# A hybrid decoder layer on one core: the split halves of the output and MLP weights are kept in DRAM from the first token block on

## The chip, the cores and the metric

The kernel runs on one core of a Trainium2 chip. The metric is the device time of one execution in microseconds, the median of several runs; the profile shows one execution of its own. The engines are called PE (TensorE, the matmuls; PEld are its weight loads), DVE (VectorE), ACT (ScalarE), POOL (GpSimd) and SP (SyncE, whose queue issues all of this kernel's DMAs).

## The reference, cut to what matters

One layer of a decoder is computed for a prompt of 2048 tokens and, beside it, for 8 sequences of 8 new tokens (the 64 "sample" tokens). All data is fp32. The width is 1024, the MLP's 2816.

```
h = rmsnorm(x, norm_mix) * (1 + sc_m) + sh_m
rq, rk, rv, rg, sq, sk, sv = split(h @ w_in)          # 3584 columns
mix = concat(retention(rq, rk, rv, rg), sb_attention(sq, sk, sv)) @ w_out
x = x + g_m * mix
h = rmsnorm(x, norm_ffn) * (1 + sc_f) + sh_f
a, bval = h @ w_up_gate, h @ w_up_val                 # 2816 columns each
ff = (silu(conv3(a)) * bval) @ w_down
x = x + g_f * ff;  y = rmsnorm(x, norm_final)
```

The shifts, scales and gates come from a small projection of a condition vector. The sample tokens attend to 2048 cached tokens each.

## The kernel before, in words

**Products in three parts.** Every large product is made with operands split in two fp32r halves: `hi` is the operand rounded to fp32r, `lo` the rest. `split` (L173) makes them with one ACT copy (L174) and one DVE subtraction, which stands in the trace under the helper line L159. `mm3` (L293) then issues hi x hi, hi x lo and lo x hi (L295 to L297). Four products with 512 moving columns share a row of weights in the token-major projections; in the feature-major ones a tile of 8 rows meets all 512 tokens of a block, so that one pair of weight halves feeds 24 matmuls of 512 columns. The last block carries the 64 sample tokens too: its feature-major products take 576 columns as two pieces of 288, and its token-major ones add a short tile (L304, L305).

**Weights.** A weight comes from DRAM as `raw`, 1 MiB (in the down projection also 512 KiB), into one of two buffers of the pool `wraw`. `w_split` (L266) turns each half of it into a pair of halves, 512 KiB each, in two of the six slots of the pool `whl`; so three pairs fit. `w_fm` (L272) yields the pairs of two feature-major tiles, `w_tm` (L288) those of two rows of a token-major projection, as they are asked for. There are 74 pairs a block in the four matrices of the change: 8 in `w_out`, 22 each in `w_up_gate` and `w_up_val`, 22 in `w_down`; `w_in` has 28 and the condition's matrix 48 pairs in all, so that there are 74 x 4 + 28 x 4 + 48 = 456 splits. The raw loads of the four matrices are 4, 11, 11 and 14 in a block.

**Blocks and order.** The prompt is cut in four blocks of 512 tokens. The first part of the kernel makes the input projections of all blocks, beside the sample's attention and the retention. Then `out_block(0)` makes the first output projection, and `ffn_block(0)` to `ffn_block(3)` run the MLP. The output projection of the next block runs between the two halves of the last down projection of the present one; at the end of that, the first two gate pairs of the next block are fetched ahead (`first_gates`). The MLPs of blocks 0 to 2 are traced side by side with the prompt's attention for blocks 1 to 3 (`_weave`), which uses PE, ACT, DVE and POOL, and loads keys and values through SP; block 3 runs alone. Inside a block the columns of the MLP come in four parts (6, 6, 6 and 4 tiles of 128), each with its gate, value and down projection.

The framework orders the instructions of each engine, places every tile in a slot of its pool and adds the semaphore waits. Each engine, and SP for the DMAs, works its instructions in order: one that waits holds all behind it. A slot is written anew only when all that read or wrote the earlier tile have ended.

Of the kernel before, what the change touches and what calls it, by code (L numbers as in the profile page):

```python
# [5 lines left out]
F32 = mybir.dt.float32  # L6
F32R = mybir.dt.float32r
# [112 lines left out]
class _Stream:  # L120
    """Traced work in steps; each step yields its share of the whole, or None while it has to wait."""

# [15 lines left out]
def _weave(streams, until=None):  # L138
    """Traces the streams side by side, each at the rate that lets all of them end together."""
    while any(s.live for s in streams) and (until is None or until.live):  # L140
        for s in sorted((s for s in streams if s.live), key=lambda s: s.got / s.total):
            if s.step():
                break
        else:
            raise RuntimeError("streams wait for each other")


def body(tc, I, O):
# [18 lines left out]
    def ld(o, i):  # L167
        dma(sp, o, i)
# [7 lines left out]

    w_in, w_out = I["w_in"][0], I["w_out"][0]
    w_ug, w_uv, w_dn = I["w_up_gate"][0], I["w_up_val"][0], I["w_down"][0]
    xp = I["x_prompt"][0]
# [84 lines left out]

    # ------------------------------------------------------------ weights
    def w_split(src, a, b, eng=dve):  # L266
# [4 lines left out]

    def w_fm(src, c0):  # L272
        raw = T(wraw, [P, 2048], F32, "raw").rearrange("p (a b) -> p a b", a=8)
        ld(raw, src[:, c0 : c0 + 256].rearrange("(k p) c -> p k c", p=P))
        for m in range(2):
            yield w_split(raw[:, :, m * P : (m + 1) * P], 8, P)

# [9 lines left out]

    def w_tm(src, r0, n, c0):  # L288
        for r, raw in w_rows(src, r0, n, c0):
            for q in range(0, raw.shape[1], 2):  # L290
                yield r + q, w_split(raw[:, q : q + 2], 2, 512)

# [6 lines left out]
    def tok_mm(ps, x, w, start, stop):  # L299
        """Rows of tokens x (hi, lo) times w; a short tile has hi and lo side by side, their rows to be added."""  # L300
        if isinstance(x, tuple):
            mm3(ps, x, w, start, stop)
        else:
            pe.matmul(ps, x, w[0], start=start, stop=False)  # L304
            pe.matmul(ps, x, w[1], start=False, stop=stop)  # L305
# [40 lines left out]
    def by_tile(tiles, k0, n):  # L346
        """The products of two rows of weights with the tiles; those of the last two tile after tile."""
        order = [(k, tile) for k in range(k0, k0 + 2) for tile in tiles]
        return sorted(order, key=lambda kt: kt[1]) if k0 == n - 2 else order

    def dense_pair(wts, acts, t, features=False):
        """Two tiles of outputs, the first half of the tokens (or features) of both before the second."""
        outs = [fm_banks(t) for _ in wts]
        for h in range(2):
            for wt, out in zip(wts, outs):
                if features:
                    for ps, c0, c1 in out:
                        fm_chunk(wt, acts, ps[:, : c1 - c0], c0, c1, range(h * 4, h * 4 + 4))
                elif t == 512:
                    fm_chunk(wt, acts, out[0][0][:, h * 256 : h * 256 + 256], h * 256, h * 256 + 256)  # L360
                else:
                    ps, c0, c1 = out[h]
                    fm_chunk(wt, acts, ps[:, : c1 - c0], c0, c1)
        return outs
# [7 lines left out]

    # ------------------------------------------------------------ norms
    def rstd_of(ss, n, scale, p=P):
# [21 lines left out]
    def half_features(x, o, n, kh, A, B, acts, hpool):  # L396
        """Half kh of the columns of normalised rows, scaled and shifted, into columns o.. as hi and lo."""
        ks = slice(kh * 4, kh * 4 + 4)
# [32 lines left out]
    def sb_norm(o, n, pl, gain, tag):  # L431
        """o: [P, n], two heads of 64 rows; returns o / rms of its head * gain. Yields between its steps."""
        w = min(P, n)
# [29 lines left out]

    # ------------------------------------------------------------ preparation
    def prep(pl, kp):
# [100 lines left out]

    # ------------------------------------------------------------ input projection
    def raw_features(hp, xT):
        """The first block's rows, normalised and transposed before the modulation is known."""
        for i, o, n in TILES + [(NT, TB, NS)]:  # L570
# [179 lines left out]

    # ------------------------------------------------------------ decode attention
    def decode(dp):
# [184 lines left out]

    # ------------------------------------------------------------ retention
    def group_norm(ps, gg, qd, pl, n):
        """ps: [n, 512], four heads, each lacking its rows' decay qd; returns the gated norm of the whole."""  # L940
        mv = T(pl, [P, HR, 2], F32, "mv")
# [155 lines left out]

    # ------------------------------------------------------------ prompt attention
    def attention(blocks, tp):
# [102 lines left out]

    # ------------------------------------------------------------ output projection and MLP
    def out_block(g, xpools, fp, samp):
        """Output projection, residual and the MLP's normalised input; xpools() gives the pool of x2."""
        t = TB + (NS if samp else 0)
# [61 lines left out]
    def ffn_block(g, x2, fp, samp, after=None):  # L1268
        """The MLP and the final norm; `after` runs between the halves of the last down projection."""
        t = TB + (NS if samp else 0)  # L1270
# [123 lines left out]
    def conv_state(fi, fp):  # L1394
        """The last rows of two tiles of gates, as rows."""
        s = T(fp, [P, 512], F32, "hf")
        ps = pz()
        for q in range(2):
            cs = T(fp, [P, 18], F32, "cvc")
            pool.tensor_copy(cs[:, 0:2], carry[:, fi + q, :])  # L1400
            pool.tensor_copy(cs[:, 2:18], scarry[:, fi + q].rearrange("p b j -> p (b j)"))
            pe.transpose(ps[:18, q * P : (q + 1) * P], cs, ident)
        act.copy(s[:18, : 2 * P], ps[:18, : 2 * P])
        cs = slice(fi * P, (fi + 2) * P)
        sv(O["conv_state_prompt"][:, cs], s[0:2, : 2 * P])
        sv(O["conv_state_sample"].rearrange("b j d -> (b j) d")[:, cs], s[2:18, : 2 * P])
# [12 lines left out]

    # ------------------------------------------------------------ the parts in their order  # L1420
    tile_pool = lambda name, bufs=1: tc.tile_pool(name=name, bufs=bufs, reuse_waits="tile")
# [85 lines left out]
class _Bufs:  # L1507
    """A pool whose tags have their own numbers of slots."""

# [9 lines left out]
class _Two:  # L1519
    """Two pools, the first for the tags given."""  # L1520

# [44 lines left out]
```

## Time and profile before

| | |
|---|---|
| runs | 3482.68, 3483.96, 3484.57 us; median 3483.96 |
| profiled execution | 3483.6 us, mean granted clock of PE 0.979 |
| last raw load of `w_out` for block 0 issued | 1233.4 us |
| first gate load of block 0 issued | 1265.1 us |
| DMA | 527.72 MB in all, mean 151 GB/s |

In the rows of groups the columns are the line, the engine, the operation, what it writes and reads, shapes and count, then busy time and the mean of one in ns, then the idle time of the engine in front of them and what ended it. In the rows of stretches they are the stretch and its length, the busy time of each engine with the number of instructions, the granted share of PE's clock, the busy share of the 16 DMA engines and the GB/s moved; where a tile is asked for, only the instructions that read or write it are counted. In the rows of waits a line gives who waited for whom, the time in total, how often, and the longest. In the rows of the timeline and of the chain: start, duration, engine, line and tiles. `whl` are the halves of weights, `raw` a weight as loaded, `act` the halves of a block's activations, `ahl` and `abe` attention's tiles, `hf`, `c`, `a` and `ff` those of the MLP, `gp` a gate of the residual.

### The profile page before, as it was taken

To read this page: it belongs to the slowest core of one execution; us is meant where nothing else is said; L and a number is where in the kernel's file an instruction comes from. 1 tells how busy PE (TensorE), PEld (TensorE's weight loads), DVE (VectorE), ACT (ScalarE), POOL (GpSimd) and SP (SyncE) were. 2 spreads that over 40 slices of the span, in tenths; PEclk is the share of its full clock that TensorE was granted. 3 is DMA by queue.
4 is the path that set the end of the run, shared out by engine and by line. 5 is a ranking of instruction groups with operands and counts; after the bars stand their busy time and mean duration, and the time that the engine had idled before them with its cause. 6 is when DMAs were issued, how large, how long until landed. Compare 5 with 4: busy or idle time off the path is not lost. (4 is left out here: it accounts for less than half of the span.)

```text
span 3483.6 us, 49595 instructions
## 1 busy us (share of the span) xinstructions
PE 3298.8 (95%) x17111; PEld 2693.4 (77%) x17111; DVE 2287.1 (66%) x3258; ACT 1777.9 (51%) x3153; POOL 1021.5 (29%) x1898
## 2 busy tenths in 40 slices
PE   7999999899999989999998999998899999899998
PEld 5887877776777768777877778777677777799997
DVE  5466666665665567777768777776877775545445
ACT  5457666554544456455556555554655553433323
POOL 3012011101433243434344333333433323221113
PEclk8999999999999989999999999999999999999999
DMA  6666776666756763443453333335333334332221
GB/s 226 229 198 193 234 230 218 221 223 211 210 178 194 246 196 103 121 121 112 121 182 118 118 118 112 106 112 181 109 118 106 112 103 136 112 107 88 83 86 65
DMA packets 406233, 527.72 MB, mean 151 GB/s; under 512 B 27830, under 2 KB 244009, under 8 KB 405982
## 3 DMA queue, kind: packets, MB, share of 16 engines
q1 hardware_dynamic: 405982, 524.55, 47.8%
q8 instruction: 136, 2.23, 0.3%
q14 instruction: 115, 0.94, 0.1%
HBM read 442.47 MB, written 81.99 MB: 151 GB/s over the span
## 5 line engine op out<-in xcount | busy, mean ns | idle before, releaser
L159 DVE TENSOR_TENSOR whl<-raw,whl 128x1024 fp32r<-128x1024 f32 x456 | 572.7, 1260 | 566.8 <-ACT whl L174 556.5
L174 ACT CAST whl<-raw 128x1024 fp32r<-128x1024 f32 x456 | 477.3, 1050 | 909.2 <-PE d L296 639.0
L295 PE MATMUL d<-act,whl 128*128 128x512 f32 (+2 forms) x2016 | 741.9, 369 | 5.5 <-ACT act L424 4.7
L297 PE MATMUL d<-act,whl 128*128 128x512 f32 (+2 forms) x2016 | 737.9, 366 | 4.6 <-DVE whl L159 4.6
L296 PE MATMUL d<-act,whl 128*128 128x512 f32 (+2 forms) x2016 | 735.7, 365 | 4.2 <-POOL act L159 2.2
L295 PEld LDWEIGHTS d<-act,whl 128*128 128x128 f32 x2016 | 385.8, 192 | 66.0 <-ACT act L424 6.7
L297 PEld LDWEIGHTS d<-act,whl 128*128 128x128 f32 x2016 | 385.4, 191 | 65.0 <-DVE whl L159 5.9
L296 PEld LDWEIGHTS d<-act,whl 128*128 128x128 f32 x2016 | 387.2, 192 | 60.9 <-POOL act L159 2.6
L295 PE MATMUL d<-whl,ff 128*128 128x512 f32 x704 | 280.9, 399 | 0.0
L296 PE MATMUL d<-whl,ff 128*128 128x512 f32 x704 | 280.0, 398 | 0.0
L297 PE MATMUL d<-whl,ff 128*128 128x512 f32 x704 | 279.9, 398 | 0.0
L295 PE MATMUL d<-whl,act 128*128 128x512 f32 x640 | 258.4, 407 | 14.0 <-DVE hf L159 10.8
L296 PE MATMUL d<-whl,act 128*128 128x512 f32 x640 | 259.0, 405 | 0.1
L297 PE MATMUL d<-whl,act 128*128 128x512 f32 x640 | 257.3, 403 | 0.0
L1138 DVE TENSOR_TENSOR_SCAN aom<-aom,acy 128x512 f32<-128x512 f32 x192 | 250.9, 1307 | 5.1 <-ACT aom L1124 4.6
L159 DVE TENSOR_TENSOR abe<-abe,aom 128x512 f32<-128x512 f32 (+2 forms) x320 | 234.3, 732 | 25.9 <-POOL abe L1128 5.1
L1162 PE MATMUL acc<-ahl,avv 128*128 128x512 f32 (+3 forms) x640 | 226.0, 413 | 17.6 <-ACT ahl L174 11.4
L1124 ACT ACTIVATE aom<-z,nb 128x512 f32<-128x512 f32 (+2 forms) x320 | 201.0, 628 | 73.4 <-PE z L1121 57.2
L1121 PE MATMUL z<-akk,aq 128*128 128x512 f32 (+3 forms) x640 | 193.4, 378 | 12.0 <-DVE scd L159 5.8
L1125 ACT ACTIVATE abe<-z,bb 128x512 f32<-128x512 f32 (+2 forms) x320 | 199.7, 624 | 0.0
L159 DVE TENSOR_TENSOR ahl<-z,ahl 128x512 fp32r<-128x512 f32 (+1 forms) x320 | 191.0, 597 | 11.4 <-ACT ahl L174 11.1
L159 POOL TENSOR_TENSOR ff<-ff,hf 128x512 f32<-128x512 f32 (+1 forms) x101 | 160.5, 1611 | 107.8 <-DVE hf L159 107.7
(289 smaller groups left out, 6219.4 us busy)
## 6 DMA issues: line engine op xcount, KB each, us to landing
raw<-in_w_in SPq DMA_DIRECT2D x56, 1024.0 KB
raw<-in_w_up_gate SPq DMA_DIRECT2D x44, 1024.0 KB
raw<-in_w_up_val SPq DMA_DIRECT2D x44, 1024.0 KB
akk<-k SPq DMA_DIRECT2D x160, 256.0 KB
page<-in_cache_k_pages SPq DMA_DIRECT2D x128, 256.0 KB
page<-in_cache_v_pages SPq DMA_DIRECT2D x128, 256.0 KB
raw<-in_w_down SPq DMA_DIRECT2D x32, 1024.0 KB
raw<-in_w_ada SPq DMA_DIRECT2D x24, 1024.0 KB
```

The costliest lines, as they stand in the source:

```text
L159: eng.tensor_tensor(o, a, b, op)
L174: act.copy(hi, src)
L295: pe.matmul(ps, sh, mh, start=start, stop=False)
L296: pe.matmul(ps, sh, ml, start=False, stop=False)
L297: pe.matmul(ps, sl, mh, start=False, stop=stop)
L1121: pe.matmul(z[:, :n], qs[g, h][:, i * P : (i + 1) * P], kk[:, c, :n], start=c == 0, stop=c == 1)
L1124: act.activation(om[:, :n], z[:, :n], AF.Sigmoid, bias=nb[:, h : h + 1], scale=-SCALE)
L1125: act.activation(be[:, :n], z[:, :n], AF.Sigmoid, bias=bb[:, h : h + 1], scale=SCALE)
L1138: dve.tensor_tensor_scan(rv, rv, rv, init, ALU.mult, ALU.bypass)
L1162: pe.matmul(accs[0][:, cs], kv[u][1][:, kt, :], m[:, cs], start=(s == g and kt == 0 and c == 0), stop=(s == 0 and kt == NT - 1 and c == 1),)
```

## The change

In block 0 each pair of halves of `w_out`, `w_up_gate`, `w_up_val` and `w_down` is written to a DRAM tile of its own (`keep`: two stores of 512 KiB). In blocks 1 to 3, and wherever the pair is asked for again, it is loaded from there into two slots of `whl` (`again`: two loads of 512 KiB); the raw load, the ACT copy and the DVE subtraction are not made. `w_in` and the condition's matrix go on as before. Docstrings and comments were dropped too.

```diff
-    w_in, w_out = I["w_in"][0], I["w_out"][0]
-    w_ug, w_uv, w_dn = I["w_up_gate"][0], I["w_up_val"][0], I["w_down"][0]
+    w_in, w_out, w_ug, w_uv, w_dn = "w_in", "w_out", "w_up_gate", "w_up_val", "w_down"
+    W = {n: I[n][0] for n in (w_in, w_out, w_ug, w_uv, w_dn)}
+    KEPT = (w_out, w_ug, w_uv, w_dn)
+    kept = {}
...
-    def w_fm(src, c0):
+    def keep(key, w):
+
+        if key[0] in KEPT:
+            t = kept[key] = T(dram, [2, P, 1024], F32, "kw")
+            for c in range(2):
+                sv(t[c], w[c].rearrange("p a b -> p (a b)"))
+        return w
+
+    def again(key, a):
+        w = []
+        for c in range(2):
+            t = T(whl, [P, 1024], F32R, "whl")
+            ld(t, kept[key][c])
+            w.append(t.rearrange("p (a b) -> p a b", a=a))
+        return tuple(w)
+
+    def w_fm(name, c0):
+        keys = [(name, c0, m) for m in range(2)]
+        if keys[0] in kept:
+            for key in keys:
+                yield again(key, 8)
+            return
         raw = T(wraw, [P, 2048], F32, "raw").rearrange("p (a b) -> p a b", a=8)
-        ld(raw, src[:, c0 : c0 + 256].rearrange("(k p) c -> p k c", p=P))
-        for m in range(2):
-            yield w_split(raw[:, :, m * P : (m + 1) * P], 8, P)
+        ld(raw, W[name][:, c0 : c0 + 256].rearrange("(k p) c -> p k c", p=P))
+        for m, key in enumerate(keys):
+            yield keep(key, w_split(raw[:, :, m * P : (m + 1) * P], 8, P))
...
-    def w_tm(src, r0, n, c0):
-        for r, raw in w_rows(src, r0, n, c0):
+    def w_tm(name, r0, n, c0):
+        if (name, r0, c0) in kept:
+            for q in range(0, n, 2):
+                yield q, again((name, r0 + q, c0), 2)
+            return
+        for r, raw in w_rows(W[name], r0, n, c0):
             for q in range(0, raw.shape[1], 2):
-                yield r + q, w_split(raw[:, q : q + 2], 2, 512)
+                yield r + q, keep((name, r0 + r + q, c0), w_split(raw[:, q : q + 2], 2, 512))
```

## The prediction, made before the result was known

> **What bounds the kernel now.** I read the head of the page first, then the split's groups in its part 5, then the stretches of the MLP half, and last who waits for whom on TensorE and on the DMA queue.
>
> ```profile
> span 3483.6 us, 49595 instructions
> PE 3298.8 (95%) x17111; PEld 2693.4 (77%) x17111; DVE 2287.1 (66%) x3258; ACT 1777.9 (51%) x3153; POOL 1021.5 (29%) x1898
> ...
> L159 DVE TENSOR_TENSOR whl<-raw,whl 128x1024 fp32r<-128x1024 f32 x456 | 572.7, 1260 | 566.8 <-ACT whl L174 556.5
> L174 ACT CAST whl<-raw 128x1024 fp32r<-128x1024 f32 x456 | 477.3, 1050 | 909.2 <-PE d L296 639.0
> ```
>
> TensorE (PE) is busy for 95% of the span. The splits that the change attacks are the largest group of VectorE (DVE), a quarter of its busy time, and a quarter of ScalarE's (ACT) too. But ACT stands idle for 909 us in front of its half of a split, most of it because the slot for the result is still being read by PE: the splits are done ahead of need, and PE sets the pace.
>
> How much PE loses, and where, is read from the stretches. With "steady" for the inside of a token block and "change-over" for the stretch from the last down projection of one block to the first gates of the next, the rows are: end of the input stage with the first output projection, steady 0, change-over 0-1, steady 1, change-over 1-2, steady 2, change-over 2-3, steady 3, tail.
>
> ```profile
> core 0: us, PE busy (x) PEld busy (x) DVE busy (x) ACT busy (x) POOL busy (x), PEclk, DMA share, GB/s
> 1159.00:1300.00 141.00, 123.53 (x655) 99.77 (x653) 83.31 (x171) 66.69 (x136) 48.88 (x107) 0.96 0.76 229
> 1300.00:1750.00 450.00, 442.72 (x2124) 356.82 (x2124) 343.92 (x436) 246.69 (x420) 173.67 (x308) 0.99 0.38 114
> 1750.00:1915.00 165.00, 147.24 (x728) 118.03 (x726) 123.69 (x164) 97.00 (x183) 68.18 (x117) 0.96 0.48 155
> 1915.00:2350.00 435.00, 428.97 (x1995) 342.46 (x1996) 333.23 (x408) 231.77 (x383) 158.08 (x275) 0.99 0.38 113
> 2350.00:2515.00 165.00, 144.19 (x696) 114.53 (x695) 121.05 (x158) 91.80 (x171) 63.84 (x110) 0.96 0.46 147
> 2515.00:2920.00 405.00, 401.26 (x1873) 321.48 (x1872) 306.16 (x369) 213.09 (x344) 139.84 (x237) 1.00 0.35 106
> 2920.00:3050.00 130.00, 118.52 (x529) 94.59 (x528) 64.30 (x97) 52.97 (x99) 38.67 (x50) 0.96 0.44 143
> 3050.00:3440.00 390.00, 390.00 (x2570) 366.40 (x2569) 190.46 (x282) 133.27 (x232) 67.61 (x175) 1.00 0.27 89
> 3440.00:3484.00 44.00, 27.81 (x126) 22.28 (x124) 23.79 (x33) 14.52 (x31) 19.56 (x25) 0.87 0.15 55
> ```
>
> In steady 3 PE is never idle, with all its splits still there: relief of DVE and ACT is worth nothing in these 390 us. In steady 1 and 2 PE is idle for 6.0 and 3.7 us. The three change-overs hold 17.8, 20.8 and 11.5 us, 50.1 together, and their clock of 0.96 costs another 0.04 of 460 us, 18.4. So from the end of block 0 to the tail no more than about 83 us can be won: 59.8 of idle time, the 18.4, and 0.01 x 435 = 4.4 for the clock in steady 1.
>
> **What is removed.** A block uses 74 pairs of weight halves in these four matrices (8 of the output projection, 22 each of gate, value and down projection). Blocks 1 to 3 drop 222 splits: 222 x 1050 = 233 us of ACT and 222 x 1260 = 280 us of DVE. Nearly all of that lies beside PE. What reaches PE is read from its waits after 1840 us:
>
> ```profile
> PE z L454 <- POOL sbr L159: 10.7, 4, 3.0
> PE d L295 <- DVE hf L159: 6.1, 3, 4.2
> PE d L297 <- DVE whl L159: 3.8, 1, 3.8
> PE d L295 <- ACT whl L174: 2.3, 1, 2.3
> PE z L295 <- ACT whl L174: 0.4, 1, 0.4
> ```
>
> PE waits directly for a split three times, 6.5 us in all; these waits end with the splits. The longest of them, and a row of the stretches around it and around the next:
>
> ```profile
> 2498.10 0.50 PE L297 MATMUL d<-act,whl 128*128 128x512 f32 x1 [3.83 <-DVE whl L159]
> ```
>
> ```profile
> 2497.00:2507.00 10.00, 8.39 (x25) 6.35 (x26) 10.00 (x10) 7.12 (x13) 6.33 (x8) 0.66 0.24 80
> 2972.00:2979.00 7.00, 5.72 (x18) 4.55 (x19) 3.58 (x3) 3.04 (x3) 0.00 (x0) 0.76 0.58 188
> ```
>
> A slow clock follows each: 10 us at 0.66 lose 3.4, 7 us at 0.76 lose 1.7. With these 5.1, 6.5 + 5.1 = 11.6 us go. The Trainium skill (TensorE: Matmul & The Clock Gate, Part 1: The HAM clock gate) says that the array's clock is halved after an idle window of about 3.4 us. By that the wait of 2.3 us would bring no slow window and only 9.9 us would go; the second row speaks against it, so the sum goes by the rows.
>
> The other waits are for ACT, DVE and GpSimd doing other work, some of it queued behind a split. How much of that queue is split is seen in the change-overs:
>
> ```profile
> 1750.00:1915.00 165.00, 111.82 (x480) 84.61 (x478) 21.61 (x18) 18.93 (x18) 0.96 0.48 155
> 2350.00:2515.00 165.00, 109.84 (x468) 84.04 (x469) 20.26 (x17) 17.86 (x17) 0.96 0.46 147
> 2920.00:3050.00 130.00, 114.55 (x484) 90.27 (x483) 19.49 (x16) 17.66 (x17) 0.96 0.44 143
> ```
>
> These are the instructions on the halves alone: 61.4 of 309.0 us of DVE's work and 54.5 of 241.8 of ACT's, about 20%. The rest of the change-overs' loss is 50.1 - 6.5 = 43.6 idle and 18.4 - 5.1 = 13.3 of clock; steady 1 and 2 have 9.7 and 4.4. Between none and all of these 71.0 us can go. I take the 20% by which the queues get shorter: 8.7 + 2.7 + 2.8 = 14.2 us. What is late next in a change-over is the chain of residual, norm and transposes, which is untouched, and GpSimd in the norm after attention (10.7 us above), untouched too.
>
> The tail begins with the last split:
>
> ```profile
> 3447.74 0.25 PE z L304
> 3448.07 1.06 ACT whl L174
> 3449.16 1.23 DVE whl L159
> 3450.38 0.61 DVE hf L159
> ```
>
> Without it the residual could start up to 2.3 us earlier, unless it waits for PE anyway. I take 1.0.
>
> **What is added in blocks 1 to 3.** 444 loads of 512 KiB straight into the 6 slots (3 pairs) that PE reads, instead of 120 loads into two raw buffers. 222 x 0.5 MiB = 116 MB more are read (and 78 MB more written in block 0), on top of these:
>
> ```profile
> HBM read 442.47 MB, written 81.99 MB: 151 GB/s over the span
> ```
>
> Steady 3 moves 89 GB/s at a share of 0.27, so full use is 330 GB/s, and a pair, 1 MiB, takes 3.2 us of it; per block of 400 to 600 us this adds 118 us of work or a share of 0.2 to 0.3, which fits. An issue costs SP 0.37 us, 148 x 0.37 = 55 us a block, beside other work. The time of one load from issue to use is bounded from below by 3.2 us and from above by the start of the kernel, where two loads of 1 MiB and others were sent at 1.93 us and the first was used at 7.92, 6.0 us later:
>
> ```profile
> 1.93 0.98 SPq L165 DMA_DIRECT2D raw<-in_w_ada  x2
> 7.92 1.99 ACT L174 CAST whl<-raw 128x1024 fp32r<-128x1024 f32 x2
> ...
> 1835.87 0.39 PE L297 MATMUL d<-whl,act 128*128 128x512 f32 x1
> 1836.00 0.37 SPq L165 DMA_DIRECT2D raw<-in_w_up_gate  x1
> 1836.10 0.40 PE L295 MATMUL d<-whl,act 128*128 128x512 f32 x1
> ```
>
> I take 5.0. Matmuls start 0.23 us apart, so a pair's 24 last 5.6 us. A load can start when PE has finished the pair three before, and must be there two pairs, 11.2 us, later: 6.2 us in hand. The raw buffers, which today stand between SP and the splits, no longer help. SP works its queue in order, so what holds it up longer than this makes PE wait:
>
> ```profile
> SPq L165 <- DVE ff L1353: 64.8, 17, 24.7
> SPq L165 <- ACT ahl L174: 43.8, 5, 13.6
> SPq L165 <- ACT hf L1403: 43.4, 11, 12.4
> ```
>
> These are SP's own waits after 1880 us. A wait for PE does no harm, since PE works through its own order and releases slots in it. Waits for ACT and DVE (stores of attention results, of conv rows, of final rows) can. Most last 3 to 9 us, but the longest exceed 6.2. Bounds: below, nothing; above, one wait of 13.6 - 6.2 = 7.4 us with 3.4 of slow clock at each of 4 places, 43 us. I take 5, nearer to nothing, because the long ones stand in change-overs and the tail, where PE is late itself.
>
> **What is added in block 0.** 148 stores of 512 KiB, 78 MB. SP waits in each for its split; behind it stand the next raw load and attention's loads. In steady 0 the share of 0.38 leaves room: 66 pairs of 1 MiB at 300 GB/s (114 / 0.38) are 231 us of the 615 to the end of the change-over, a share of 0.4 more. A slot now comes free when its store has landed too, but that has three pairs, 16.8 us. The tight place is the first output projection, at 0.76 and 229 GB/s already: 8 pairs, 8.4 MB, are 28 us at 301 GB/s, and the share becomes 0.96. Bounds: nothing, and one pair's stores (3.5 us) ahead of each of the 4 raw loads, 14 us. I take 2.
>
> **The sum.** -11.6 - 14.2 - 1.0 + 5 + 2 = -19.8 us. The profiled execution's 3483.6 becomes 3463.8; the median of the runs, 3483.96, stands 0.4 above it, so 3464.
>
> **The rivals.** *Hidden anyway.* The change-overs are held by the chain of norm and transposes, not by queue length; only the direct waits go and the new costs eat them: -11.6 + 7 = -5, 3479. For it speaks that PE's largest waits name POOL sbr and DVE hf, not splits. Against it, DVE is busy for 121 to 124 of 165 us in two of the change-overs, and each split stands 1.26 us in its queue.
>
> *Late halves, slower.* With three pairs as the only stock, loads behind SP's waits arrive late. Each hold of 13.6 us costs 7.4 + 3.4 = 10.8; it takes 2.3 of them to eat the gain of 24.8 that remains without my allowance of 5 (26.8 less block 0's 2), so from three on the kernel is slower. With four, 3484 - 24.8 + 43 = 3502. For it: the maxima above. Against: the queue's order follows PE's for everything that PE releases, and the typical wait is inside 6.2 us.
>
> *PE has room of its own.* The Trainium skill (Perfetto Trace Analysis, Identifying the Most-Contended Engine) says to judge TensorE by the busy share of its weight loads, not of its matmuls. As a mechanism of this kernel: if feeding holds PE back inside its busy time, steady 1 and 2 could rise from a PEld share of 0.79 (342.46 of 435) to steady 3's 0.94 (366.40 of 390), and 840 x (1 - 0.79 / 0.94) = 134 us would go: 3350. Against it: the back-to-back starts 0.23 us apart above stand in a block with attention and splits, and in the tail's chain the last matmul of steady 3 has the same 0.25. Steady 3 loads more often because it streams 288 columns per load instead of 512.
>
> **How the numbers follow.** Forecast 0.62, hidden anyway 0.18, late halves 0.18, room of PE 0.02. A measurement of this kernel tells about 0.2%, 7 us, from no change. So faster 0.64, same 0.18, slower 0.18. The forecast's own range takes half of the 71 us (-35.5) with no new waits: -49, 3434; and none of them with new waits of 15: 3489. Leaving out the tips, and reaching halfway into the slower rival, I give 3438 to 3492.
>
> **What would show it.** Right: in the waits of PE no more whl from ACT or DVE after 1880 us, only DMA; 234 splits left in part 5; HBM written 160 MB and read 559; steady 3 unchanged at 390; change-overs together some 20 us shorter, with 35 to 40 us of PE idle instead of 50; DVE's share in steady 1 down from 77% to about 60%. Wrong: PE waiting for DMA whl over 15 us in all, above all behind SP's waits for ACT or DVE; change-overs as long as before; or steady 0 or the first output projection longer by over 5 us.

## The result, and the profile after

The changed kernel takes 3511.68 us in the median (3509.8 to 3514.61), the kernel before beside it 3484.27 (3482.68 to 3486.44): a ratio of 1.0082, 95% interval 1.0068 to 1.0096, some 28 us slower. The profiled executions are 3508.1 and 3483.6 us long. The forecast was 3464, some 20 us faster than before, with a range of 3438 to 3492; the kernel became slower instead, and its time lies 20 us above the range.

The page of the kernel after, with the head, the two halves of a split and the traffic:

```profile
span 3508.1 us, 49855 instructions
...
PE 3306.3 (94%) x17111; PEld 2697.7 (77%) x17111; DVE 2041.3 (58%) x3036; ACT 1568.2 (45%) x2931; POOL 962.8 (27%) x1898
...
HBM read 558.86 MB, written 159.59 MB: 205 GB/s over the span
...
L159 DVE TENSOR_TENSOR whl<-raw,whl 128x1024 fp32r<-128x1024 f32 x234 | 293.7, 1262 | 267.0 <-ACT whl L174 256.1
...
L174 ACT CAST whl<-raw 128x1024 fp32r<-128x1024 f32 x234 | 244.2, 1050 | 319.4 <-PE d L323 243.4
```

The change does what it says: 234 splits are left, DVE is busy for 246 us less and ACT for 210, and the bytes are those forecast. PE is busy for 7.5 us more in a span that is 24.5 longer, so 17 us are new idle time.

The stretches of the MLP half, with bounds moved so that each holds the same part of the work as the row of the kernel before (first output projection, steady 0, change-over 0-1, and so on to the tail):

```profile
core 0: us, PE busy (x) PEld busy (x) DVE busy (x) ACT busy (x) POOL busy (x), PEclk, DMA share, GB/s
1156.00:1320.00 164.00, 137.73 (x704) 110.18 (x703) 90.11 (x181) 72.54 (x150) 50.58 (x112) 0.92 0.78 256
1320.00:1760.00 440.00, 434.13 (x2075) 348.51 (x2074) 336.26 (x426) 240.50 (x406) 170.42 (x302) 1.00 0.76 259
1760.00:1927.00 167.00, 147.00 (x728) 117.46 (x727) 111.04 (x151) 84.27 (x168) 62.87 (x118) 0.96 0.66 216
1927.00:2362.00 435.00, 428.40 (x1997) 344.95 (x1997) 268.74 (x351) 180.20 (x328) 136.39 (x274) 0.99 0.59 183
2362.00:2528.00 166.00, 145.00 (x694) 113.84 (x693) 104.71 (x139) 74.94 (x152) 63.01 (x109) 0.95 0.62 201
2528.00:2933.50 405.50, 401.95 (x1874) 323.57 (x1873) 244.89 (x314) 162.09 (x290) 116.89 (x238) 0.99 0.56 176
2933.50:3076.00 142.50, 120.17 (x545) 96.68 (x544) 44.29 (x81) 36.46 (x82) 35.17 (x48) 0.92 0.56 191
3076.00:3466.00 390.00, 388.31 (x2553) 364.21 (x2552) 121.69 (x221) 74.17 (x171) 66.30 (x176) 1.00 0.50 172
3466.00:3508.10 42.10, 27.89 (x126) 22.34 (x124) 22.42 (x31) 12.62 (x29) 18.69 (x25) 0.86 0.31 107
```

The steady parts are as long as before, with DVE down to 62% in steady 1 (268.74 of 435). Two stretches are longer: the first output projection (164 us; 1159 to 1310, 151 us, hold the same work in the kernel before) and the last change-over (142.5 against 130).

Stretches with hand-set bounds are rough to 1 or 2 us. A sharper measure counts work: 11,902 matmuls read a tile of weights (`whl` or `raw`) in every kernel of this study, and the start of the n-th of them can be set against its start in the kernel before. The table gives by how many us each stretch is longer (+) or shorter (-); its stretches end, in the kernel before, at 1137.3 us (input stage), 1363.1, 1737.2, 1940.4, 2321.6, 2529.3, 2906.0, 3098.8, 3429.4 and the span's end. The first output projection lies in the second of them; "first gates" of each block are in the change-overs. The last column is the sum without the input stage, in which no kernel changes the work.

```
             input  out   steady  c-o   steady  c-o   steady  c-o   steady  tail   without
             stage  proj    0     0-1     1     1-2     2     2-3     3             input
after         -2.9  13.1   -0.0   1.9   -0.5    1.5    0.2   12.8   -0.0   -1.5     27.4
e1            -3.0   0.5   -0.1  -0.3   -0.6   -5.1   -1.1   -3.4    0.0   -1.2    -11.3
e2            -5.4  12.4   -0.0   4.9   -0.0    3.7   -1.4    9.3    0.0   -0.9     28.0
e3            -8.7  14.1   -0.1   1.3   -1.4   -0.9   -1.5   -3.0   -0.0   -0.4      8.0
e4            -8.4  15.2   -0.1  -2.4   -2.3   -6.5   -1.0    2.2    0.0   -1.5      3.6
e5             3.9   1.0   -0.1  -1.7   -3.1   -6.3   -1.4   -7.3    0.0   -1.2    -20.1
e6             2.1   6.6    2.9   2.0    0.6    1.6    0.2   13.7    0.0   -1.3     26.3
e7             2.1  13.7   -0.1   2.8   -0.5    1.3    0.1    8.2    0.0   -1.5     24.0
e8            -6.9   1.0    0.1  -1.9   -0.5   -5.2   -2.6   -2.1    0.0   -1.2    -12.4
e9             5.2  -0.0   -0.1   2.5   -0.5   -5.5   -2.5    3.8    0.0   -1.1     -3.4
e10          -12.4   0.5   -0.1  -1.8   -0.5   -7.9   -2.6   -5.4   -0.0   -1.1    -18.8
e11           -8.3   0.5   -0.1   1.4   -0.5   -5.4   -2.5   -2.5   -0.0   -1.2    -10.1
e12           -8.4  10.3   -0.0  -1.0   -0.4   -5.4   -2.6   -2.0    0.0   -1.5     -2.5
```

The input stage alone differs by 17 us between single profiled executions (-12.4 to +5.2), so whole spans compare badly and the last column better: +27.4 here against some +28 from the timed runs. A row is still one execution of its kernel: e1, e8, e11 and e12, whose blocks 1 to 3 are alike but for e8's gate rows, differ by up to 3 us in the sum of the columns from change-over 0-1 on. The loss has two places, 13.1 and 12.8 us, and the change-overs won nothing.

**The last change-over.** The waits of PE for weights after 1880 us, kernel after:

```profile
PE d L322 <- issue: 17.1, 1, 17.1
PE d L324 <- DMA whl<-kw: 1.1, 1, 1.1
PE d L322 <- DMA whl<-kw: 0.6, 1, 0.6
```

No wait for a split is left, as forecast, but one of 17.1 us is new. It has no releaser in the view; what PE reads there are activations and the first halves of the last output projection. The semaphore events of the trace tell which came last: the last load of activations had landed at 2971.0 us, the first half landed at 2987.18, and PE began at 2987.27. PE's timeline around it, and then SP's:

```profile
2969.77 0.40 PE L324 MATMUL d<-whl,ff 128*128 128x512 f32 x1
2987.27 1.19 PE L322 MATMUL d<-whl,act 128*128 128x512 f32 x2 [17.10 <-issue]
```

```profile
2965.56 0.52 SPq L165 DMA_DIRECT2D act<-mx  x1
2972.92 0.33 SPq L165 DMA_DIRECT2D gp<-gp  x1
2973.30 0.42 SPq L165 DMA_DIRECT2D smp<-ms  x1
2973.77 1.85 SPq L165 DMA_DIRECT2D ff<-in_x_prompt  x4
2975.67 1.02 SPq L165 DMA_DIRECT2D ff<-in_x_sample  x1
2976.73 6.37 SPq L165 DMA_DIRECT2D whl<-kw  x6
```

```profile
SPq L165 <- DVE hf L159: 6.8, 1, 6.8
```

SP stands for 6.8 us before `gp<-gp`, a gate whose slot DVE has yet to read (`DVE hf`), and all loads of halves come behind it. PE, which ran out of work at 2970.2, begins 10.5 us after the first of them is issued. Over that time the DMA engines are full:

```profile
2976.70:2987.30 10.60, 0.03 (x1) 0.06 (x1) 0.00 (x0) 0.72 (x2) 2.61 (x3) 0.50 1.01 330
```

SP in the kernel before, in the same place:

```profile
2930.43 0.37 SPq L165 DMA_DIRECT2D raw<-in_w_out  x1
...
2960.05 0.33 SPq L165 DMA_DIRECT2D gp<-gp  x1
...
2961.98 1.16 SPq L165 DMA_DIRECT2D raw<-in_w_out  x2
```

The same hold was there (SP reached `gp<-gp` at 2960.05). But a raw load of the output projection had gone out at 2930.43, 30 us ahead of it, into a raw buffer that was free. The halves have no buffer of that kind: their slots come free only as PE works the down projection, and so the framework puts their loads after the activations, the gate and the rows of x.

**The first output projection.** The raw loads of `w_out` after the first two, in the kernel before and in the kernel after:

```profile
1201.69 0.38 SPq L165 DMA_DIRECT2D raw<-in_w_out  x1
1233.43 0.57 SPq L165 DMA_DIRECT2D raw<-in_w_out  x1
```

```profile
1254.44 0.38 SPq L165 DMA_DIRECT2D raw<-in_w_out  x1
1277.22 0.70 SPq L165 DMA_DIRECT2D raw<-in_w_out  x1
```

They go out 53 and 44 us later, behind the stores of the first four and the first six pairs. And the DMA engines had no room. Twenty microseconds at about the same part of the work, kernel before and kernel after:

```profile
1243.00:1263.00 20.00, 20.00 (x89) 16.09 (x89) 7.38 (x10) 7.26 (x16) 6.23 (x11) 1.00 1.00 253
```

```profile
1240.00:1260.00 20.00, 13.24 (x52) 9.94 (x50) 6.06 (x10) 6.58 (x16) 7.62 (x17) 0.85 1.05 340
```

Before the change PE was busy throughout while the DMA engines were already at a share of 1.00. Their mean of 0.76 over the stage hid that. With the stores PE loses a third of the stretch, 6.8 us, and all of it while it waits for attention's keys, a load that has nothing to do with the weights:

```profile
PE z L1148 <- DMA akk<-k: 6.8, 2, 5.4
```

### The profile page after: what moved, and what is told of

It reads as the page before. It is cut to its first block, busy times and chain, and to the rows that moved or that the text cites. A ratio compares the mean times of both kernels' runs of the same rounds, so it can differ in the third digit from the quotient of the medians.

```text
span 3508.1 us, 49855 instructions
## 1 busy us (share of the span) xinstructions
PE 3306.3 (94%) x17111; PEld 2697.7 (77%) x17111; DVE 2041.3 (58%) x3036; ACT 1568.2 (45%) x2931; POOL 962.8 (27%) x1898
## 5 line engine op out<-in xcount | busy, mean ns | idle before, releaser
L159 DVE TENSOR_TENSOR whl<-raw,whl 128x1024 fp32r<-128x1024 f32 x234 | 293.7, 1262 | 267.0 <-ACT whl L174 256.1
L174 ACT CAST whl<-raw 128x1024 fp32r<-128x1024 f32 x234 | 244.2, 1050 | 319.4 <-PE d L323 243.4
L174 ACT CAST ahl<-z 128x512 fp32r<-128x512 f32 (+1 forms) x320 | 167.6, 524 | 389.4 <-PE z L1177 380.1
L322 PE MATMUL d<-whl,act 128*128 128x512 f32 x640 | 257.3, 410 | 17.6 <-issue 17.1
L1322 DVE SCALAR_TENSOR_TENSOR c<-a,vecs,c 128x512 f32<-128x512 f32 x176 | 134.1, 762 | 213.9 <-ACT c L1319 163.2
L159 DVE TENSOR_TENSOR hf<-d,gp 128x512 f32<-128x512 f32 x160 | 108.4, 683 | 179.1 <-PE d L324 159.0
```

Of the source, the lines that this page charges most:

```text
L159: eng.tensor_tensor(o, a, b, op)
L174: act.copy(hi, src)
L322: pe.matmul(ps, sh, mh, start=start, stop=False)
L1322: dve.scalar_tensor_tensor(c[:, :TB], a[:, j : j + TB], cw(j), c[:, :TB], ALU.mult, ALU.add)
```

## The experiments

The first theory was this: the two places are the whole loss, and relief of ACT and DVE is worth nothing. Its rivals: the added bytes cost wherever they stand; or relief is worth 20 us and late loads eat it.

**e1, the output projection raw everywhere.**

```diff
-    KEPT = (w_out, w_ug, w_uv, w_dn)
+    KEPT = (w_ug, w_uv, w_dn)
```

> The output projection's weights are loaded raw and split in all four blocks, as before the change; the other three matrices are kept (66 of 74 pairs a block). Theory (two places): the 26 us that the change lost up to the last block were lost in the first output projection of block 0 (13 us: stores in SP's queue ahead of raw and attention loads) and in the last change-over (13 us: the loads of the output projection's halves behind a store or load that waits for VectorE); relief of ACT and VectorE is worth next to nothing. Then this kernel comes back to the kernel before: 3480 to 3487. Rival (bytes): what costs is the added traffic wherever it stands; 66 of 74 pairs are left, so about 24 of the 27 us stay: 3505 to 3511. Rival (relief eaten): relief is worth some 20 us and late loads eat it elsewhere; without the two places 3460 to 3475.

Measured: 3468.48 us beside 3479.09 for the kernel before, ratio 0.9968 (0.9956 to 0.9981). It is faster than both kernels, inside the range of the rival *relief eaten*. The two places are gone (0.5 and -3.4 us in the table), and the theory is wrong on relief: the kernel gains 11 us, 5.1 of them in change-over 1-2 and 3.4 in the last, whose clock goes from 0.96 to 1.00:

```profile
2911.00:3035.00 124.00, 113.82 (x531) 91.19 (x530) 52.51 (x87) 43.59 (x88) 35.44 (x46) 1.00 0.48 166
```

**e2, the output projection alone.**

```diff
-    KEPT = (w_out, w_ug, w_uv, w_dn)
+    KEPT = (w_out,)
```

> Only the output projection's weights are kept (8 of 74 pairs a block); the other three matrices are raw and split everywhere. Theory (two places): the whole loss is here with a ninth of the change: about +26 us, 3503 to 3513. Rival (bytes): 8 of 74 of the cost, +3 us: 3484 to 3490. Between the two if the stores of the first block and the loads of the last are not both due to this matrix alone: 3490 to 3503.

Measured: 3511.57 us, ratio 1.0101 (1.0086 to 1.0116). A ninth of the change costs as much as all of it, as the theory had it. It costs in the first output projection (12.4) and in all three change-overs (4.9, 3.7, 9.3), not in the last alone.

**e3, stores that nobody loads.** `keep` stores each pair the first time and registers nothing, so that blocks 1 to 3 load raw and split.

```diff
-        if key[0] in KEPT:
-            t = kept[key] = T(dram, [2, P, 1024], F32, "kw")
+        if key[0] in KEPT and key not in seen:
+            seen.add(key)
+            t = T(dram, [2, P, 1024], F32, "kw")
```

> Block 0 stores all halves as in the change, and no later block loads one: blocks 1 to 3 load raw and split as before. Theory (two places): block 0's part alone, +13 us: 3493 to 3500, with the last change-over as in the kernel before. Rival (bytes): 78 MB of the 195 MB added, so some 10 us as well, but spread over the whole of block 0 and not in its output projection. Rival (the stores cost nothing, all is in the later loads): 3482 to 3488.

Measured: 3489.84 us, ratio 1.0041 (1.0025 to 1.0056), by which it is some 14 us slower, as the theory had it (its range was set beside 3484 for the kernel before, which takes 3479 here). The table has 14.1 in the first output projection and -0.1 in steady 0, where most of the other 132 stores go out at no cost. It also has -6 us in later stretches that should be as before; no run explains these.

**e5, one half loaded and used twice**, on top of e1.

```diff
+        t = T(whl, [P, 1024], F32R, "whl")
+        ld(t, kept[key][0])
+        t = t.rearrange("p (a b) -> p a b", a=a)
+        return t, t
```

> As e1_w_out_raw, but blocks 1 to 3 load only the high half of each kept pair and use it for the low half too, so the low half's product is left out of the result's meaning while the matmuls stay the same: no splits, half the added loads, and six pairs of stock instead of three. It shows the most that relief of ACT and VectorE can bring once loads are early. Theory (relief is worth next to nothing): within 4 us of e1_w_out_raw, 3476 to 3486. Rival (relief eaten by late loads): 3455 to 3470, some 15 or more under e1_w_out_raw.

Measured: 3461.11 us, ratio 0.9947 (0.9934 to 0.9961). Its results are not the layer's; only its time is of use. The relief of 66 pairs a block is worth 20.1 us in the table, and e1 keeps 11.3 of them. I read the difference of 8.8 as what the loads of both halves cost at three pairs of stock, where the rival expected 15 or more; the timed runs have 7 us. So both sides held a part: two places, and a real relief under them.

**What makes the first output projection long: the order of SP's queue, or bytes?** In e6 the stores go out on ScalarE's queue.

```diff
-                sv(t[c], w[c].rearrange("p a b -> p (a b)"))
+                dma(act, t[c], w[c].rearrange("p a b -> p (a b)"))
```

> The whole change, but the 148 stores of block 0 are issued from ScalarE's queue instead of SP's; bytes and slots as in the change. The stores cost 13 us in the first output projection, where the third raw load of the output projection left SP 21 us later than before. Theory (order of SP's queue): with the stores out of SP's queue the raw load goes out at its old place and the first output projection costs 0 to 4 us instead of 13; the last change-over stays as long as in the change; total 3492 to 3501. Rival (bytes): the DMA engines are full there whichever queue sends, so the 13 us stay: 3505 to 3515. Rival (ScalarE is held by its own stores): longer than the change, over 3515.

Measured: 3508.39 us beside 3481.03, ratio 1.0069 (1.0051 to 1.0088), inside the interval of the change. The raw loads are nearly back in their places (1203.8 and 1240.5 us), and the stage still costs 6.6 with 2.9 in steady 0, 9.5 together. Theory and rival both had a part, the rival the larger one. This run alone does not tell the bytes from ScalarE being held by its own stores; the next one leaves ScalarE free.

**e12, the stores of `w_out` on GpSimd's queue, unused**, on top of e1: all the bytes of the stage, SP's order untouched, ScalarE free.

```diff
+        elif key[0] == w_out and key not in seen:
+            seen.add(key)
+            t = T(dram, [2, P, 1024], F32, "kw")
+            for c in range(2):
+                dma(pool, t[c], w[c].rearrange("p a b -> p (a b)"))
```

> As e1_w_out_raw, but block 0 also stores the output projection's halves in full (16 stores, 8.4 MB), from GpSimd's queue, and nobody loads them: all the bytes of the change in the first output projection, with the raw loads of the output projection in SP's queue at the places that they have in e1. In the change that stage cost 13 us more than before; with the stores on ScalarE's queue it cost 6.6, and 2.9 more in the steady part behind it. Theory (half order, half bytes): the stage costs 5 to 8 us more than in e1: ratio 0.998 to 0.9995. Rival (bytes alone do it): 11 to 14 us more, ratio 0.9995 to 1.001. Rival (order alone; the 6.6 were ScalarE's): 0 to 3 us more, ratio 0.9962 to 0.998.

Measured: 3476.26 us beside 3480.38, ratio 0.9995 (0.9984 to 1.0007); the stage is 10.3 us longer than before and 9.8 longer than in e1, between the theory and the first rival. The same twenty microseconds:

```profile
1235.00:1255.00 20.00, 15.02 (x56) 11.68 (x55) 4.62 (x6) 3.48 (x5) 4.71 (x7) 0.83 1.02 386
```

DMA is full, and PE loses 5 of 20 us with SP's order as in e1. Its two longest waits in the stage:

```profile
PE acc L1194 <- ACT ahl L174: 6.6, 2, 5.5
PE d L327 <- DMA act<-mx: 5.0, 1, 5.0
```

The second is a load of activations that comes late. Behind the first, too, stands a transfer: ahead of it ACT waits 3.45 us for a store of value rows (`out_v_rows_prompt`) to land, where in e1 it does not wait. GpSimd, which now waits for splits ahead of its stores, ends none of PE's long waits (1.0 us in the longest, against 2.1 before), so nothing points to its hold. By two queues, then, 9.1 (e6 less e1, steady 0 included) to 9.8 of the 12.6 us that separate the change from e1 in this stage are bytes. The rest I put down to the place of the raw loads in SP's queue, by subtraction alone. The Trainium skill (DMA: Bandwidth & Descriptors, Issuing engines are not separate DMA queues) says that transfers of all issuing engines run on the same 16 DMA engines. The trace agrees: with the stores on GpSimd's queue the share stands at 1.02, and a load that SP issued is waited for 5.0 us.

**e11, thin stores from SP's queue**: as e12, with `sv(t[c][:, :128], ...)`, an eighth of the bytes and all the waits.

> As e1_w_out_raw, but block 0 also stores 64 of the 512 KiB of each half of the output projection from SP's queue, and nobody loads them: as many stores and as many waits of SP for splits in the first output projection as in the change, an eighth of the bytes. Theory (bytes in a place where the DMA engines are full): the first output projection costs 0 to 3 us more than in e1 instead of 13: ratio 0.996 to 0.998. Rival (SP's waits for the splits): 8 to 13 us more than e1: ratio 0.999 to 1.001.

Measured: 3472.54 us beside 3479.98, ratio 0.9979 (0.9968 to 0.999); the stage costs 0.5 us, as in e1. SP waits 36 us for splits in this stage (48 in the change), and these waits by themselves cost nothing. The thin stores did not push the raw loads back either (third and fourth at 1199.2 and 1222.2 us), so this run doesn't separate bytes from the order that they bring about; e12 does.

**What makes the last change-over long: SP's hold, or the stock?** In e7 the last output projection's gate rows get slots that are idle then, on top of the whole change.

```diff
-        gm = T(fp, [P, 512], F32, "gp")
+        own = spool and i == 0
+        gm = T(spool if own else fp, [P, 512], F32, "hf" if own else "gp")
```

> The whole change, but the gate rows of the last output projection land in slots of their own that are idle at that time, so that SP no longer waits there for VectorE (6.8 us) ahead of the loads of the halves. Theory (SP held by one wait): TensorE's wait of 17.1 us in the last change-over shrinks by 7 or more, to at most 10, and the kernel is 7 to 12 us faster than the change: 3496 to 3502. Rival (the loads are late anyway, since their slots come free too late or the DMA engines are full): the wait stays at 14 us or more and the kernel within 3 us of the change: 3505 to 3512.

Measured: 3510.49 us, ratio 1.0087 (1.0074 to 1.01), by the timed runs no faster than the change. PE's wait, and SP around it, and the DMA engines over the time:

```profile
PE d L322 <- issue: 11.7, 1, 11.7
```

```profile
2973.89 2.36 SPq L165 DMA_DIRECT2D ff<-in_x_prompt  x4
2977.06 0.51 SPq L165 DMA_DIRECT2D ff<-in_x_sample  x1
2977.61 5.80 SPq L165 DMA_DIRECT2D whl<-kw  x6
```

```profile
2956.00:2988.00 32.00, 20.30 (x88) 16.01 (x86) 6.36 (x10) 4.77 (x11) 11.32 (x9) 0.88 1.01 343
```

The hold is gone, and the wait shrinks by 5.4 us to 11.7, between what the two expected. This execution is some 6 us later in its work: PE runs out at 2976.3, and the first half leaves SP 1.3 us after that, where it was 6.6 us in the change. It still takes 10.3 us to land, behind 4 MB of activations and 2 MB of x, which together with the halves keep the DMA engines full for 32 us. By the table the hold was 4.6 us of the loss (12.8 less 8.2), which is within the noise of the timed runs.

**e4, five pairs of stock.** Two of every five pairs in blocks 1 to 3 land in the idle raw buffers.

```diff
+        turn[0] += 1
+        both = T(wraw, [P, 2048], F32, "raw") if turn[0] % 5 in (1, 3) else None
         for c in range(2):
-            t = T(whl, [P, 1024], F32R, "whl")
+            if both is None:
+                t = T(whl, [P, 1024], F32R, "whl")
+            else:
+                t = both[:, c * 1024 : (c + 1) * 1024].bitcast(F32R)
```

> The whole change, but two of every five pairs of halves in blocks 1 to 3 land in the two raw buffers, which are idle then: five pairs of stock instead of three. Theory (stock): the loads of blocks 1 to 3 go out two pairs, 11 us, earlier, so that the lateness in the change-overs (26 us for the output projection, some 9 for the other matrices) shrinks by half or more; block 0's 13 us stay: 3478 to 3495. Rival (SP's order): the loads stand behind the same waits in SP's queue, and the stock is eaten in the same holds: 3500 to 3512.

Measured: 3488.66 us, ratio 1.0029 (1.0017 to 1.004). The theory holds: block 0's part stays (15.2), and the change-overs go from 1.9, 1.5 and 12.8 to -2.4, -6.5 and 2.2. By the table two pairs of stock win 23.8 us, by the ratios of the timed runs 18. What is left in the last one is seen in SP's queue and in PE's waits:

```profile
2928.82 0.32 SPq L165 DMA_DIRECT2D whl<-kw  x1
2954.20 0.33 SPq L165 DMA_DIRECT2D gp<-gp  x1
2955.60 0.58 SPq L165 DMA_DIRECT2D whl<-kw  x1
```

```profile
PE d L328 <- DMA whl<-kw: 6.8, 1, 6.8
```

The first half goes out 25 us ahead of the gate, as the raw load did, but its low half behind it.

**e8, e1 with the gate rows of e7.**

> As e1_w_out_raw (the output projection's weights raw in all blocks), with the last output projection's gate rows in idle slots of their own as in e7_own_gates. Where the halves are not loaded behind it, the wait for the gate rows should cost nothing: within 3 us of e1_w_out_raw, 3464 to 3474 on a chip where the kernel before takes 3479. If that wait held up other loads too: 3 to 8 us under it.

Measured: 3469.73 us, ratio 0.9974 (0.9964 to 0.9985), as e1: where nothing needed stands behind the hold, it is free.

**e9, five pairs, `w_out` stored by block 1** (`keep` passes over its first sight of a `w_out` pair).

> As e4_five_pairs (two of five pairs of halves land in the raw buffers), but the output projection's halves are stored by block 1 and loaded by blocks 2 and 3; block 0 stores only the other three matrices. Theory (the stores cost in the first output projection because the DMA engines are full there, at a share of 0.76 before the change, and cost nothing where they have room): e4 stood at 1.0029 with 15 us lost in that one stage, which go: 3461 to 3470 on a chip where the kernel before takes 3481, under e1_w_out_raw's ratio of 0.9968 or equal to it. Rival (a store costs wherever it stands in SP's queue ahead of a raw load): the loss moves to block 1's output projection, 3476 to 3488.

Measured: 3480.8 us beside 3479.98, ratio 1.0002 (0.999 to 1.0014). The time is in the rival's range, but not for its reason. The first output projection is as before (-0.0), and the stores cost some 4 us in change-over 0-1 (2.5 where e10 has -1.8), so that the rival holds for that part. The larger part is lost where `w_out` is loaded: 2 us in change-over 1-2 (-5.5 where e10 has -7.9), and 9 in the last one (3.8 where e10 has -5.4). The theory overlooked that.

**e10, five pairs, `w_out` raw everywhere.**

> As e1_w_out_raw, with five pairs of stock: the output projection raw in every block, and the raw buffers shared between its loads and two of five pairs of the others. Theory (stock): the 9 us by which e1 stood above e5_one_half were late loads, and most go: ratio 0.993 to 0.996. Rival (shared buffers): the raw loads of the output projection lose their head start of some 30 us in the change-overs because the buffers are taken by pairs, and what is won is lost there: ratio 0.996 to 1.001.

Measured: 3468.29 us, ratio 0.9962 (0.9944 to 0.9979). By time it can't be told from e1, and both expectations touch the interval. In the table it has -18.8 against e1's -11.3, close to e5's -20.1 with all the bytes of e1, which speaks for the stock; that the timed runs don't show these 7 us stays open. e1 and e10 are the fastest of the kernels that compute the layer in full, 0.3 to 0.4% below the kernel before.

## Why the prediction was wrong

- **What bounds the kernel: right.** In the kernel after, the steady parts changed by 0.5 us or less each; in the other kernels without these splits steady 1 and 2 are shorter by 3.1 us at most. Relief there is worth little, and the 134 us of the rival *PE has room of its own* are out.
- **What is removed: right in kind, a little large.** The forecast was 26.8 us for 74 pairs a block, 23.9 for 66 by the count of pairs; the runs gave 20.1 (e5) and 18.8 (e10) for 66. No run separates the 11.6 us of direct waits from the 14.2 of shorter queues, of which the 20% was a guess. *Hidden anyway* is out: relief was worth more than its 11.6 us. The tail gave 1.5 for 1.0. Of what was to be seen, the 234 splits, the bytes, the waits without a split, steady 3 and DVE's 62% (for about 60) came true; the change-overs, together 16.2 us longer instead of 20 shorter, did not. Of the signs of being wrong, PE's waits for halves (18.8 us, over 15) and the first output projection (13.1 us, over 5) came.
- **What is added in blocks 1 to 3: the step that failed first.** A load that takes 5.0 us, with 6.2 us in hand, became a term of 5 us in the sum. The runs give 8.8 for the three matrices (e5 to e1), and for `w_out` the 38.7 between the change and e1 less 12.6 in block 0, that is 26.1 us net of the relief of its own 8 pairs: together 34.9 us for 5. Two things were wrong in that step. The load of a pair was bounded by 6.0 us from the start of the kernel, where little else is under way; in the last change-over six loads went out in 6.4 us into full DMA engines, and the first needed 10.5 us to land. And the text says that the raw buffers "no longer help", but prices it at nothing: their loss is the 30 us by which a raw load ran ahead of the gate's hold and of the rush of activations, and giving the buffers back (e4) took 3.6 - 27.4 = -23.8 us.
- **"The long ones stand in change-overs ..., where PE is late itself": wrong.** PE waited 17.1 us there. The rival *late halves* had the sign and, with 3502, the nearest time, but its price was for four of SP's holds of 13.6 us, so that the nearness is luck; the one hold was 4.6 us by the table, the lost lead and the full DMA engines were the rest.
- **What is added in block 0: the step that failed next.** I took 2 us of a bound of 14; it was 13.1. The rate of 301 GB/s and the share of 0.96 were means over 141 us, in which 20 us stood at 1.00 already. The bound itself was nearly met, by luck: it was worked out for stores that stand ahead of raw loads in SP's queue, and by e6 and e12 some 9 to 10 us are bytes whichever queue sends them. In steady 0, where the share had room, the stores were free, as forecast.
- **The sum:** -20.1 of relief, +8.8 and +26.1 of late loads, +12.6 of stores are 27.4, against the forecast's -19.8. These terms are differences between kernels, so they add up by construction. In the range, the lower tip doesn't: 11.6, 35.5 and 1.0 are 48, not 49; nothing hangs on it.

## What to carry to other kernels

A buffer between DRAM and the slot that the matmul reads is also a head start: before it is bypassed, read how far ahead its loads leave the queue, and at which rush they would stand instead. Price added transfers by the fullest 20 us of a stage, not by its mean share. When a large change gains in most places and loses in one, look for the ninth of it that loses: here leaving the output projection as it was turned 28 us of loss into 11 us of gain.

## What the runs showed of the hardware that was not expected

A DMA share of 1.0 is no rate: full stretches moved 253, 340 and 386 GB/s above, with packets of 1.7, 2.0 and 2.1 KB in the mean, so my 330 GB/s for "full use" was neither a bound nor a mean.

SP also waits for the landing of transfers that the issue has no use for. In the last change-over of e7 (2950 to 3000 us) the loads of `act`, x and halves carry eight semaphores in turn, and SP holds each issue until the transfer eight places ahead of it, the last one with the same semaphore, has landed:

```profile
SPq L165 <- DMA whl<-kw: 4.5, 1, 4.5
SPq L165 <- DMA act<-mx: 4.2, 7, 0.9
SPq L165 <- DMA ff<-in_x_prompt: 2.8, 3, 1.3
```

In this case the slow clock after the longest wait lasted no longer than after short ones. After the wait of 17.1 us, kernel after:

```profile
2987.00:2989.00 2.00, 1.73 (x4) 1.33 (x5) 0.00 (x0) 0.00 (x0) 0.00 (x0) 0.50 1.03 410
2989.00:2991.00 2.00, 2.00 (x6) 1.52 (x6) 0.00 (x0) 0.00 (x0) 0.00 (x0) 0.50 1.02 406
2991.00:2993.00 2.00, 2.00 (x10) 1.59 (x9) 0.00 (x0) 0.00 (x0) 0.00 (x0) 0.90 0.46 178
```

Half speed for some 4 us costs 2 us, where the prediction charged 3.4 for a wait of 7.4. The prediction's two rows, after waits of 3.8 and 2.3 us, lose 3.4 and 1.7 us, which at half speed are 6.8 and 3.4 us.
